# The order of a recurrent mixer's stages: second group's inverse and keys before the first group's chunks, first output projection before the second group's chunks

## The chip, the cores and the metric

The kernel runs on one core of one Trainium2 chip. The metric is the device time of one execution in microseconds (us), the median of several runs. The profiled execution is one further run, with its own time.

The engines are called PE (TensorE, matrix products), DVE (VectorE), ACT (ScalarE), POOL (GpSimd) and SP (SyncE, which issues DMAs here). Each takes its instructions strictly in the order in which they stand in its queue, and waits on semaphores for the others.

## The reference

A trunk of two layers over 256 tokens of width 1024. Each layer is a half-weighted SwiGLU feed-forward, a mixer, and a second feed-forward, each behind an RMS norm. The change concerns the mixer of the second layer, a gated delta recurrence with 16 heads of 64:

```python
r, k, v = xr @ w_r, xk @ w_k, xv @ w_v          # xr, xk, ...: token-shift lerps of h
w = -softplus(-(w0 + tanh(xw @ w1) @ w2)) - 0.5  # decay
a = sigmoid(a0 + (xa @ a1) @ a2)
g = sigmoid(xg @ g1) @ g2                        # gate
# per head, over the tokens:
sa = S @ a_t
S = S * w_t + sa * b_t + v_t * k_t
y_t = S @ r_t
y = group_norm(y) + sum(r * k * r_k) * v
return (y * g) @ w_o
```

## The kernel before

The 256 tokens are two halves of 128, the 1024 columns of the mixer two *groups* of 512 (8 heads each). The recurrence is computed in chunks of 64 tokens: inside a chunk the steps are solved by an inverse of a triangular matrix, and from chunk to chunk a 64x64 state per head is carried. All four chunks of one group are one chain; the two groups are independent of each other until the output projection.

The work of this mixer is cut into *stages*, each a Python call that emits its instructions. `ORDER` (line 32) is a string of stage names; `trunk` runs them one after the other in that order (the table of names is the dictionary `do` in it). From this program order a scheduler lays out the queue of each engine, and fills one stage's waits with instructions of neighbouring stages. So ORDER sets only roughly what stands where, and the engines' queues are shown below where they matter. The names, with G the group and h the token half:

- `k`, `r`/`R`, `v`/`V`: the three projections (`c_project`); the capital is the second group's columns. The weights come as fp32 and are split into a high and a low part (ACT L213, DVE L218 or POOL L216), and each product is three matmuls (L223 to L225). `v` also copies the values by chunk (ACT L665).
- `L`, `g`: the small loras; `g` is the gate's (`c_gate`): lerps whose product is on ACT (L593) and whose add is on POOL (L595), and matmuls on L603.
- `oG`, `pGh`, `DG`: operands of group G (keys normalised, decays); ACT, DVE and POOL work with transposes on PE.
- `bGh`, `kGh`: Gram blocks of the chunks (`c_gram`, PE L719 and L726, masked by DVE on L802), first those with b (tile `gb`), then those with k (tile `gk`).
- `sG`: `c_blocks` stores the diagonal blocks of `gb` to DRAM (`ds`, SP L819) and loads them in another layout as `L` (L824). `tG`: `c_substitute` solves these small blocks on DVE (L839 to L849) and stores the result (`xd`, `xtd`, L855). `lG`: `c_load` (L867) loads it back, per half as X (tiles `xx` for group 0, `hT` for group 1) and its transpose (`b`). `dGh`: `c_rest` builds the inverse of a whole chunk from it, in four rounds of PE (L719) and DVE (one L881, three L890).
- `vGh`: the bonus term (`c_bonus`): POOL products (L693), a DVE sum (L900), and a POOL add (L902).
- `cGh`: the two chunks of half h (`c_chunk`). A chunk is a chain, done for two pairs of banks: PE makes W, ACT copies it (L929), PE makes u, DVE copies it (L934), PE makes the new state, DVE scales it (L946, L949); the output leaves by ACT (L959).
- `WG`: the output weights of group G (`c_weights`), 8 loads of 256 KB by SP (L1025) through three `hn` buffers, each split by ACT (L289) and DVE (L290) into tiles that hold operands of group 0 before (`b`, `k`, `a`, `gb`, `gk` for W0, and `xx`, `hT`, `k`, `V`, `ka`, `rc` for W1).
- `PGh`: what follows the recurrence (`c_post`): gate (PE L977, ACT L979), centring by a matmul (PE L985), square and variance (ACT L989, DVE L991, L992), norm (DVE L998, L999), transposes (PE L1001) and a split.
- `OhG`: the output projection of half h with the rows of group G (`c_out`), 24 matmuls (L223 to L225), accumulated over G into one accumulator per half; `ah`: adds it to the trunk and begins the last feed-forward for half h (norm, with transposes on PE L268).
- `X`, `Y`: give and take back memory of the weight rings of the feed-forward (`rings_open("base")` at Y), after which its weights (`raw`) can be loaded.

```python
            for n in ORDER.split():
                do[n]()
```

Of the kernel before, what the change touches and what calls it, by code (L numbers as in the profile page):

```python
# [28 lines left out]
QB = (0, 0)  # L29
QV = (0, 0)  # L30
NPT = 2
ORDER = 'L k o0 r p00 p01 R b00 b01 g s0 o1 p10 p11 v V t0 D0 D1 X b10 b11 s1 l0 d00 d01 k00 k01 t1 v00 v01 l1 c00 c01 k10 k11 v10 v11 d10 d11 W0 P00 P01 c10 c11 P10 O00 W1 P11 O01 O10 Y a0 O11 a1'
BIG = 8
ORDER_AB = 'I0 N1 K0 Q0 S0 P0 E0 F0 I1 K1 Q1 S1 P1 E1 F1 O0 B0 O1 B1'
ABP = (2, 3, 0, 1)
# [1009 lines left out]
def trunk(tc, A, out, stop=None):  # L1045
    with ExitStack() as ctx:
# [56 lines left out]
        with t.pool("pre") as t.pre:  # L1103
# [18 lines left out]
            def tail(h):  # L1122
                t.add_acc(h, t.cs["acc", h])
                t.ffn_begin(S[3], h, 3)
# [13 lines left out]
            for G in range(2):  # L1138
# [16 lines left out]
                do[f"a{G}"] = lambda h=G: tail(h)  # L1155
            for n in ORDER.split():
                do[n]()
# [23 lines left out]
```

## Time and profile before

| | us |
| --- | --- |
| median of 3 runs | 1120.92 (1120.82 to 1122.24) |
| profiled execution, its own time | 1116.97 |
| its span | 1115.2 |
| PE busy | 1048.2 (94%) |
| DVE busy | 638.6 (57%) |
| ACT busy | 501.6 (45%) |
| POOL busy | 216.7 (19%) |

The mean granted clock of PE is 0.981 of full speed. The span is the time from the first to the last instruction, and 1.77 us of the execution lie around it. A busy share is a mean over the whole span; the stages of the mixer that the change moves lie between about 700 and 925 us of it. In a timeline, a row has the start, the duration, the engine, the source line and the tiles of one or several equal instructions, and in brackets how long the engine was idle before and which engine's instruction ended that.

### The profile page before, as it was taken

What the parts mean: (1) busy time and instruction counts of PE and PEld (TensorE: products, weight loads), DVE (VectorE), ACT (ScalarE), POOL (GpSimd) and SP (SyncE); (2) the same over time, 40 slices, a digit from 0 to 9 for tenths busy, and PEclk for the clock granted to TensorE, in tenths of its full rate; (3) what the DMA queues carried; (4) which work ended last, traced back from release to release, by engine and by line L of the source; (5) the groups of instructions that cost most, each with busy time, mean ns of one, the idle gap of its engine ahead of it and who ended that gap; (6) DMA issues with size and microseconds to landing.
All of it is one profiled execution on the core that took longest, in us unless ns stands there. A gap on an engine that the chain in (4) does not pass through costs nothing.

```text
span 1115.2 us, 16407 instructions
## 1 busy us (share of the span) xinstructions
PE 1048.2 (94%) x6332; PEld 859.9 (77%) x6332; DVE 638.6 (57%) x922; ACT 501.6 (45%) x804; POOL 216.7 (19%) x203
## 2 busy tenths in 40 slices
PE   6999999999999999989999999998685899999998
PEld 5888887778788888778888877886684777888886
DVE  6655555665655554754556546787454648554542
ACT  6544444564544443544444435756023326543440
POOL 3101110341201010111011111635200523100100
PEclk9999999999999999999999999999798999999999
DMA  8765664552765554646556444651323027645631
GB/s 294 258 202 175 221 191 157 181 189 80 231 199 178 189 193 147 222 160 205 185 172 210 148 138 152 192 157 55 74 60 112 24 95 244 235 163 190 195 127 38
DMA packets 73695, 185.07 MB, mean 166 GB/s; under 512 B 24081, under 2 KB 24721, under 8 KB 73617
## 3 DMA queue, kind: packets, MB, share of 16 engines
q1 hardware_dynamic: 70304, 178.19, 49.6%
q10 hardware_dynamic: 3312, 5.83, 1.7%
q8 instruction: 50, 0.82, 0.3%
q14 instruction: 29, 0.23, 0.1%
HBM read 180.32 MB, written 3.67 MB: 165 GB/s over the span
## 4 chain that ended last, share of the span: by engine, by line
PE 82%; DVE 6%; DMA 4%; POOL 3%; issue 2%; ACT 2%; SPq 1%; ACTq 0%; DVEq 0%; POOLq 0%
PE gu L224 14%; PE gu L223 14%; PE gu L225 14%; PE acc L223 10%; PE acc L224 10%; PE acc L225 10%; PE tp L336 2%; PE acc L719 2%; DMA hn<-w_rkvo 1%; DMA row<-gain 1%; DVE wlo L218 1%; PE gu L719 1%; ACT whi L213 1%; PE acc L268 1%; DVE hn L262 1%
## 5 line engine op out<-in xcount | busy, mean ns | idle before, releaser
L218 DVE TENSOR_TENSOR wlo<-raw,whi 128x1024 fp32r<-128x1024 f32 x261 | 345.4, 1330 | 184.3 <-ACT whi L213 180.2
L213 ACT CAST whi<-raw 128x1024 fp32r<-128x1024 f32 x306 | 319.2, 1050 | 209.4 <-DMA raw<-w_gu 94.2
L223 PE MATMUL gu<-whi,xh 128*128 128x512 f32 x704 | 279.8, 398 | 1.6 <-ACT whi L213 1.6
L224 PE MATMUL gu<-wlo,xh 128*128 128x512 f32 x704 | 279.3, 397 | 0.8 <-DVE wlo L218 0.8
L225 PE MATMUL gu<-whi,xl 128*128 128x512 f32 x704 | 278.3, 396 | 0.0
L216 POOL TENSOR_TENSOR wlo<-raw,whi 128x1024 fp32r<-128x1024 f32 x45 | 109.0, 2423 | 607.3 <-ACT whi L213 573.7
L223 PEld LDWEIGHTS gu<-whi,xh 128*128 128x128 f32 x704 | 133.1, 189 | 28.9 <-ACT whi L213 2.0
L224 PEld LDWEIGHTS gu<-wlo,xh 128*128 128x128 f32 x704 | 133.1, 189 | 27.7 <-DVE wlo L218 1.2
L225 PEld LDWEIGHTS gu<-whi,xl 128*128 128x128 f32 x704 | 133.1, 189 | 26.8
L223 PE MATMUL acc<-whi,ah 128*128 128x512 f32 x352 | 138.5, 394 | 1.9 <-ACT ah L289 1.7
L224 PE MATMUL acc<-wlo,ah 128*128 128x512 f32 x352 | 137.3, 390 | 0.0
L225 PE MATMUL acc<-whi,al 128*128 128x512 f32 x352 | 130.8, 391 | 0.0
L331 ACT ACTIVATE t<-gu,rh 128x256 f32<-128x256 f32 x88 | 41.3, 471 | 97.2 <-PE gu L225 96.7
L290 DVE TENSOR_TENSOR al<-tp,ah 128x256 fp32r<-128x256 f32 x88 | 36.9, 420 | 82.7 <-ACT ah L289 82.7
L289 ACT CAST ah<-tp 128x256 fp32r<-128x256 f32 x88 | 32.3, 367 | 111.6 <-PE tp L336 107.0
L332 DVE SCALAR_TENSOR_TENSOR t<-t,gu 128x256 f32<-128x256 f32 x88 | 36.6, 418 | 75.8 <-ACT t L331 75.0
L223 PEld LDWEIGHTS acc<-whi,ah 128*128 128x128 f32 x352 | 66.1, 188 | 17.4 <-ACT ah L289 3.4
L224 PEld LDWEIGHTS acc<-wlo,ah 128*128 128x128 f32 x352 | 66.1, 188 | 14.4
L225 PEld LDWEIGHTS acc<-whi,al 128*128 128x128 f32 x352 | 65.9, 188 | 14.3
L224 PE MATMUL acc<-wlo,xh 128*128 128x512 f32 x160 | 65.2, 408 | 0.2 <-DVE wlo L218 0.2
L223 PE MATMUL acc<-whi,xh 128*128 128x512 f32 x160 | 63.3, 410 | 0.7 <-ACT xh L289 0.5
L225 PE MATMUL acc<-whi,xl 128*128 128x512 f32 x160 | 62.7, 398 | 0.1
(487 smaller groups left out, 1111.7 us busy)
## 6 DMA issues: line engine op xcount, KB each, us to landing
raw<-w_gu SPq DMA_DIRECT2D x176, 512.0 KB, 4.5
raw<-w_dn SPq DMA_DIRECT2D x88, 512.0 KB, 4.3
raw<-w_rkvo SPq DMA_DIRECT2D x24, 512.0 KB, 3.6
row<-gain ACTq DMA_DIRECT2D x22, 256.0 KB, 4.2
raw<-w_qp SPq DMA_DIRECT2D x8, 512.0 KB, 4.3
raw<-w_out SPq DMA_DIRECT2D x8, 512.0 KB, 3.6
hn<-w_rkvo SPq DMA_DIRECT2D x16, 256.0 KB, 2.8
ch<-chan SPq DMA_DIRECT2D x10, 256.0 KB, 5.1
```

Of the source, the lines that this page charges most:

```text
L213: nc.scalar.copy(out=hi, in_=raw)
L216: nc.gpsimd.tensor_tensor(out=lo, in0=raw, in1=hi.bitcast(F32), op=ALU.subtract)
L218: nc.vector.tensor_tensor(out=lo, in0=raw, in1=hi.bitcast(F32), op=ALU.subtract)
L223: mm(out, xh, wh, start=start, stop=False)
L224: mm(out, xh, wl, start=False, stop=False)
L225: mm(out, xl, wh, start=False, stop=stop)
L289: self.nc.scalar.copy(out=hi, in_=src)
L290: self.nc.vector.tensor_tensor(out=lo, in0=src, in1=hi.bitcast(F32), op=ALU.subtract)
L331: nc.scalar.activation(out=t, in_=gu[:, :256], func=AF.Tanh, scale=rh)
L332: nc.vector.scalar_tensor_tensor(out=t, in0=t, scalar=1.0, in1=gu[:, :256], op0=ALU.add, op1=ALU.mult)
L336: nc.tensor.transpose(ps[:, j, :], t[:, j * 128:(j + 1) * 128], self.ident)
L719: self.nc.tensor.matmul(out[rs], a[rs], b[rs], start=start, stop=stop)
```

## The change

One line is changed, the string that orders the stages of the recurrent mixer.

```diff
--- before.py
+++ after.py
@@ -29,7 +29,7 @@
 QB = (0, 0)
 QV = (0, 0)
 NPT = 2
-ORDER = 'L k o0 r p00 p01 R b00 b01 g s0 o1 p10 p11 v V t0 D0 D1 X b10 b11 s1 l0 d00 d01 k00 k01 t1 v00 v01 l1 c00 c01 k10 k11 v10 v11 d10 d11 W0 P00 P01 c10 c11 P10 O00 W1 P11 O01 O10 Y a0 O11 a1'
+ORDER = 'L k o0 r p00 p01 R b00 b01 s0 o1 p10 p11 v g V t0 D0 D1 X b10 b11 s1 l0 d00 d01 k00 k01 t1 k10 v10 v00 v01 l1 d10 k11 c00 c01 v11 d11 W0 P00 P01 O00 c10 c11 P10 O10 Y W1 P11 O01 a0 O11 a1'
 BIG = 8
 ORDER_AB = 'I0 N1 K0 Q0 S0 P0 E0 F0 I1 K1 Q1 S1 P1 E1 F1 O0 B0 O1 B1'
 ABP = (2, 3, 0, 1)
```

Three things move. The gate's lora `g` goes from in front of `s0` to behind the projection `v`. The second group's inverse and keys (`k10`, `v10`, `d10`, `k11`) go ahead of the first group's chunks `c00` and `c01`. The output projection of token half 0 with group 0 (`O00`) goes ahead of the second group's chunks `c10` and `c11`, and `O10` and `Y` ahead of `W1` and `P11`. The set of instructions is the same.

SP's queue, at the stores and loads around the two substitutions (`ds`, `L`: `c_blocks`; `xx` and `b`: `c_load(0)`, halves 0 and 1). Before:

```order
L867 DMA xx_6757<-xd 64x512 x2
L819 DMA ds<-gb_6668 64x8x64 x2
L867 DMA b_5783<-xtd 64x512 x2
L867 DMA xx_6762<-xd 64x512 x2
L867 DMA b_5786<-xtd 64x512 x2
L819 DMA ds<-gb_6711 64x8x64 x2
L824 DMA L<-ds 32x16x16 x4
```

and now:

```order
L867 DMA xx_6757<-xd 64x512 x2
L819 DMA ds<-gb_6668 64x8x64 x2
L867 DMA b_5783<-xtd 64x512 x2
L819 DMA ds<-gb_6711 64x8x64 x2
L867 DMA xx_6762<-xd 64x512 x2
L867 DMA b_5786<-xtd 64x512
L824 DMA L<-ds 32x16x16 x4
```

The second store of `ds` moved ahead of two pairs of loads; half of one pair now stands behind the loads of `L`.

PE's queue in the first chunk of group 0 (`W`, `u`, `kt`, `bt`, `gk` are c00's; `hT`, `b_6259` are d10's). Before:

```order
L719 MATMUL gu<-hT_7064,gb_6668 64x64 x9
L719 MATMUL acc_7108<-W,b_5783 64x64 x4
L719 MATMUL acc_7115<-V_6520,kt_6950 64x64
L719 MATMUL acc_7091<-u,bt_6133 64x64 x2
L719 MATMUL acc_7091<-V_6520,kt_6950 64x64 x2
L719 MATMUL acc_7091<-u,bt_6133 64x64 x2
L719 MATMUL acc_7115<-V_6520,kt_6950 64x64
L719 MATMUL acc_7125<-gk_6939,V_6520 64x64 x2
```

and now (`gu<-tmp`, `ms<-tmp` and `tp<-tmp` are d10's, `a_6216,k_6215` is k11's):

```order
L719 MATMUL acc_7275<-W,b_5783 64x64 x2
L719 MATMUL gu<-tmp 64x64 x8
L719 MATMUL ms<-tmp 64x64 x8
L719 MATMUL acc_7258<-u,bt_6133 64x64 x2
L719 MATMUL acc_7258<-V_6472,kt_6950 64x64 x2
L719 MATMUL acc_7258<-u,bt_6133 64x64 x2
L719 MATMUL acc_7275<-W,b_5783 64x64 x2
L719 MATMUL tp<-tmp 64x64 x8
L719 MATMUL gu<-tmp 64x64 x8
L719 MATMUL gu<-a_6216,k_6215 64x128 x8
L726 MATMUL ms<-ident,k_6215 64x64 x8
L719 MATMUL tp<-a_6216,k_6215 64x128 x8
```

Rounds of d10 and the first Gram blocks of k11 now stand between the W, u and state products of the first chunk.

PE's queue at the end of the mixer, at P11's first transposes (`ident,tmp`; P11's centring stands some rows ahead of each piece). Before:

```order
L223 MATMUL acc_8242<-gk_7681,xh_7746 128x512
L224 MATMUL acc_8242<-gk_7681,xh_7746 128x512
L225 MATMUL acc_8242<-gk_7681,xl_7747 128x512
L223 MATMUL acc_8242<-gk_7682,xh_7746 128x512
L224 MATMUL acc_8242<-gk_7682,xh_7746 128x512
L225 MATMUL acc_8242<-gk_7682,xl_7747 128x512
L268 MATMUL acc_8285<-ident,hn 128x128 x4
L268 MATMUL acc_8293<-ident,hn 128x128 x4
L1001 MATMUL ms<-ident,tmp 128x128 x2
L223 MATMUL acc_8241<-xx_8139,xh_8202 128x512
L224 MATMUL acc_8241<-xx_8139,xh_8202 128x512
```

and now:

```order
L224 MATMUL acc_7762<-rc_8204,xh_8124 128x512
L225 MATMUL acc_7762<-ka_8203,xl_8125 128x512
L268 MATMUL acc_8285<-ident,hn 128x128 x4
L223 MATMUL gu<-whi,xh_8273 128x512
L224 MATMUL gu<-wlo,xh_8273 128x512
L268 MATMUL acc_8293<-ident,hn 128x128 x4
L225 MATMUL gu<-whi,xl_8275 128x512
L223 MATMUL gu<-whi,xh_8273 128x512
L224 MATMUL gu<-wlo,xh_8273 128x512
L225 MATMUL gu<-whi,xl_8275 128x512
L1001 MATMUL ms<-ident,tmp 128x128 x2
```

Before, 22 output matmuls stood between the centring and P11's first transposes; now eight do, with six of the feed-forward (`whi`, `wlo`) behind the norm's transposes (`ident,hn`).

## Rows read from the trace of the kernel before

**Rows 1.** The page, part 4: the chain that ended last, share of each engine.

```profile
PE 82%; DVE 6%; DMA 4%; POOL 3%; issue 2%; ACT 2%; SPq 1%; ACTq 0%; DVEq 0%; POOLq 0%
```

**Rows 2.** Busy us of PE, weight loads, DVE, ACT, GpSimd; clock; DMA, by stretch.

```profile
740.00:760.00 20.00, 19.42 (x89) 14.25 (x89) 17.76 (x46) 13.47 (x31) 4.63 (x5) 1.00 0.45 115
860.00:880.00 20.00, 14.13 (x266) 11.85 (x266) 14.52 (x31) 7.02 (x17) 12.53 (x12) 0.78 0.13 42
871.26:919.95 48.69, 46.00 (x576) 37.18 (x576) 25.64 (x58) 12.99 (x35) 15.98 (x21) 1.00 0.21 66
920.00:930.00 10.00, 7.67 (x29) 6.02 (x30) 10.00 (x10) 7.07 (x11) 6.27 (x6) 0.83 0.52 161
```

**Rows 3.** The same columns (PE, weight loads, clock), instructions of line L603 alone.

```profile
736.00:743.00 7.00, 4.37 (x32) 3.80 (x32) 1.00 0.51 146
```

**Rows 4.** Timeline of SP's DMA issues: start, us, engine, line, operation, tiles, count.

```profile
792.10 1.23 SPq L867 DMA_DIRECT2D b<-xtd  x2
793.44 1.29 SPq L819 DMA_DIRECT2D ds<-gb  x2
```

**Rows 5.** Timeline of DVE; in brackets the idle time before and its releaser.

```profile
787.92 0.69 DVE L802 TENSOR_TENSOR gb<-gu,m_si 128x512 f32<-128x512 f32 x1 [0.62 <-PE gu L719]
...
801.37 0.16 DVE L839 TENSOR_TENSOR pr<-L,XL 128x2 f32<-128x2 f32 x1 [6.43 <-DMA L<-ds]
...
814.69 0.69 DVE L849 TENSOR_REDUCE XL<-tmp 128x64 f32<-128x512 f32 x1
...
846.86 0.29 DVE L934 COPY u<-acc 128x128 f32<-128x128 f32 x1 [0.17 <-PE acc L719]
```

**Rows 6.** Timeline of GpSimd (POOL), the second group's bonus chain.

```profile
781.53 1.28 POOL L902 TENSOR_TENSOR vb<-vb,ch 128x512 f32<-128x512 f32 x1 [5.47 <-DMA ch<-chan]
```

**Rows 7.** Timeline of PE: k01's Gram, d10's start, d11, c10's start.

```profile
815.76 1.09 PE L719 MATMUL acc<-a,k 64*64 64x128 f32 x16 [1.55 <-DVE b L890]
816.68 0.63 PE L726 MATMUL acc<-ident,k 64*64 64x64 f32 x16
817.15 1.04 PE L719 MATMUL acc<-a,k 64*64 64x128 f32 x16
...
824.42 0.69 PE L719 MATMUL gu<-hT,gb 64*64 64x64 f32 x8 [0.23 <-DMA hT<-xd]
...
862.55 1.12 PE L719 MATMUL gu<-tmp 64*64 64x64 f32 x16 [5.00 <-DVE tmp L890]
...
871.26 0.45 PE L719 MATMUL ms<-W,b 64*64 64x64 f32 x8 [0.61 <-ACT W L929]
```

**Rows 8.** Timeline of ACT: a weight split, a P01 copy, c10's first W.

```profile
862.46 0.62 ACT L289 CAST V<-hn 128x512 fp32r<-128x512 f32 x1 [1.01 <-DMA hn<-w_rkvo]
...
869.45 0.60 ACT L989 ACTIVATE tmp<-acc 128x512 f32<-128x512 f32 x1 [2.10 <-PE acc L985]
...
870.93 0.28 ACT L929 COPY W<-tp 128x128 f32<-128x128 f32 x1
```

**Rows 9.** Timeline of PE: P11, end of the output projection, start of the feed-forward.

```profile
904.41 1.05 PE L985 MATMUL gu<-centre,Pt 128*128 128x128 f32 x8
...
911.31 0.38 PE L1001 MATMUL ms<-ident,tmp 128*128 128x128 f32 x2
...
919.33 0.40 PE L224 MATMUL acc<-rc,xh 128*128 128x512 f32 x1
919.56 0.39 PE L225 MATMUL acc<-ka,xl 128*128 128x512 f32 x1
921.55 0.51 PE L223 MATMUL gu<-whi,xh 128*128 128x512 f32 x1 [1.61 <-ACT whi L213]
...
923.27 0.80 PE L224 MATMUL gu<-wlo,xh 128*128 128x512 f32 x1 [0.77 <-DVE wlo L218]
923.86 0.63 PE L225 MATMUL gu<-whi,xl 128*128 128x512 f32 x1
924.29 0.63 PE L223 MATMUL gu<-whi,xh 128*128 128x512 f32 x1
```

## The prediction

> **What bounds the kernel now.** I read the chain of waits first: of the chain that ended last, 82% is TensorE (PE) [rows 1]. So a re-ordering can pay only where PE does not work, and the second view, the busy time of each engine by stretch, says where that is [rows 2]: from 740 to 760 us PE is busy 19.42 of 20 us, from 871.26 to 919.95 it is busy 46.00 of 48.69, but from 860 to 880 only 14.13 of 20, at a granted clock of 0.78. All stages that the new order moves lie between 736 and 925 us. The rest of the kernel is the same code with the same neighbours, so I take it at its old time.
>
> The third view is the timeline of single engines. It gives three places where PE waits for a chain that the order decides:
> - Group 1's inverse (stages s1, t1, l1). SP, the sync engine's DMA queue, stores the second `ds` half at 793.44 [rows 4], though its Gram block was ready on DVE at 788.61 (787.92 and 0.69) [rows 5]. It was held by the loads of c_load(0) that stand before it in the queue. The substitution starts when L lands (801.37, DVE idle 6.43 before) and ends at 815.38 [rows 5]; d10 begins on PE at 824.42 [rows 7].
> - The start of group 1's chunks. PE waits 5.00 us for one add of c_rest at 862.55 and begins c10 at 871.26 [rows 7]. Its first W copy on ACT (870.93) comes after the P00 and P01 copies, one of which waited 2.10 us for PE at 869.45 [rows 8], and after the last split of output weights.
> - The tail. P11's centring matmul starts at 904.41 and its transposes at 911.31; PE fills the 6.9 us between with output-projection matmuls, and goes on with them to 919.95 (919.56 and 0.39) [rows 9].
>
> **The change, part by part** (its profiled execution is 1116.97 us, 3.95 under the median of the runs, 1120.92; I make the sum against the first).
>
> 1. *Gate lora behind the v projection.* Its 32 matmul records are PE's work for 4.4 us [rows 3], and these go from in front of group 0's values. At most 4.4 us are gained. At least nothing: DVE, whose adds feed the same stretch, is busy 17.76 of 20 us there [rows 2], and the substitution t0 ends in DVE's order, not PE's. I take 1.8, a little under the middle, since DVE has only 2.2 us free in that stretch. The lerp's last add on GpSimd now stands in group 1's bonus chain, right behind an instruction that waits 5.47 us for a DMA and that, at the same 128x512, takes 1.28 us [rows 6]; I take 1.2 for the add. The Gram block behind this chain in DVE's order is then 0.4 to 1.2 us later against t0's end, which is covered: SP reaches its store only later still (next part). If that cover goes, it costs 1.2.
>
> 2. *SP's order.* The second `ds` store now has one load pair in front of it in place of three (an xx and a b pair move behind). The step from such a pair to the next issue is 1.34 us, 792.10 to 793.44 [rows 4]: 2.6 us gained. The loads that move back belong to d01; they still start before 794, and d01 comes behind d00. Together with part 1, L lands 4.4 us earlier, the substitution ends at about 811.0, and d10 starts at about 820.4, 4.0 us earlier (0.4 kept back for the GpSimd add). Bounds: 0 (gb late by the GpSimd add and by PE's order) and 7.0 (2.6 plus all of 4.4).
>
> 3. *d10, k10, k11 in front of c00.* PE now runs eight groups of d10 inside and ahead of the first chunk, each of 16 records of 64x64, 0.47 us by the step from 816.68 to 817.15 [rows 7]: 3.8 us. Of k11 there are two groups of 0.92 (815.76 to 816.68) and one of 0.47: 2.3 us. Before, 1.7 us of d10 stood there. So 4.4 us of PE come in front of the first state update, of which I count 4.0, because some lies in the chunk's own waits. That takes back all that part 2 gained: c01 ends where it ended, near its last u copy at 846.86 [rows 5]. Bounds: 0 (all in gaps) and 6.5 (four rounds that each wait a full hop to DVE, 1.6 us by the wait of 1.55 on c_rest's add at 815.76 [rows 7]).
>
> 4. *The start of c10.* The output weights land in tiles of group 0's operands, so they still follow c01. What changes is ACT's and DVE's order: P00's copies now stand between the splits, and d11's adds ahead of the last ones, so the 5.00 us wait at 862.55 and the 2.10 us wait at 869.45 fall away. W now stands before the last two splits, right behind the one of V, which ends at 863.08 (862.46 and 0.62). Four copies for P00 and P01 of 0.6 us go in front of it (865.5), c10's first matmul comes 0.33 us behind W as before (871.26 less 870.93) [rows 7, 8], and 0.5 for the rest of their waits on PE: c10 starts at 866.3 in place of 871.26, 5.0 us earlier. Bounds: 0 (the copies pull in their old waits) and 7.3 (W at 863.6, one copy behind V).
>
> 5. *From c10 to the end of the output projection.* Counted by rows, PE has the same instructions to do on both sides: 46.0 us, with 2.7 us of waits before [rows 2]. New is how little stands under P11. Of the output matmuls between its centring and its transposes, only eight are left, at 0.233 us (919.33 to 919.56 [rows 9]), 1.9 us, in place of 22. The last output matmul of token half 0 also moves to right before its norm, whose transposes PE must wait for. The 6.9 us are thus covered by 1.9 and 0.8 of centring: 4.2 us bare. With 1.3 us at c10's start: 866.3 + 46.0 + 5.5 = 917.8, against 919.95: 2.1 us gained. Bounds: the bare time may be 0 (feed-forward matmuls fill it) or 6.
>
> 6. *Start of the feed-forward.* PE idles 1.61 and 0.77 us at 921.55 and 923.27 and then steps at 0.43 us per matmul, 923.86 to 924.29 [rows 9]. With weights released a little earlier I take back half of the idle time, 1.2 us; bounds 0 and 2.4.
>
> Sum: 2.1 + 1.2 = 3.3 us off, 1113.7 for a profiled execution, **1117.6 us** as a median. A measurement of this kernel tells a change of about 0.2%, 2.24 us, from none.
>
> The clock speaks against the change. The rows show it: after those two waits the same matmul steps at 0.43 us in place of 0.233 [rows 9], with the granted clock of 920 to 930 at 0.83 [rows 2]; eight such steps cost 1.6 us. A bare wait of 4.2 us in front of the last output matmuls can do the same there: the sum would be 3.3 less 1.6, 1.7 us gained, 1119.2. The Trainium skill, in "TensorE: Matmul & The Clock Gate", section "HAM oscillation — how this bites in real kernels", says that a PE that waits for data between bursts falls back to its lower clock and pays the climb each time. The trace agrees in the stretch behind 921.55. Whether the new wait under P11 does so is not shown here.
>
> **The rivals.**
> - *No change.* The tail gives the lead back: the bare P11 wait at 4.2 us with the slow steps behind it (1.6), and nothing gained at the feed-forward's start (1.2). 3.3 − 1.6 − 1.2 = 0.5 us gained, 1120.4. For it: from 871 to 920 PE is nearly full, so only 2.7 us of waits can go there, and the order brings in a new one. Against it: the 7.1 us of waits that part 4 takes away lie before this stretch.
> - *Slower: the inverse of half 0 chokes the first chunks.* d10's rounds stand in DVE's order between the u copies of c00. If each costs its hop, 6.5 us are lost in part 3 in place of 4.0, and if the GpSimd add of part 1 and DVE's fill leave nothing of part 1, c01 ends 1.8 + 2.5 = 4.3 us later. The output weights wait for its tiles, so all of part 4 moves: the gain of 3.3 becomes a loss of 1.0, and with the slow steps 2.6, and with nothing at the feed-forward's start 3.8: 1124.7. It decides against the change once c01 ends after about 850.2. For it: PE waited on c_rest's adds before, 1.55 us at 815.76 and 5.00 at 862.55 [rows 7]. Against it: the long one of these came from splits that stood between, and none do in c00.
> - *Much faster: the P11 wait is filled.* Feed-forward matmuls of the first weight block do stand between P11's centring and its transposes in PE's order. If the norm of half 0 is ready for them, the 4.2 us go: 7.5 us gained, 1113.4. Against it: half 0's last output matmul now stands just before, and the norm's chain over ACT and DVE starts only there.
> - *The change doesn't do what it says* is excluded for the order itself; the order of instructions on PE, SP, ACT and DVE differs as listed above.
>
> **How the numbers follow.** Forecast 0.42 (own range 1115.5 to 1119.5), no change 0.24, slower 0.21, much faster 0.13. The forecast lies 1.1 us inside the bound for faster (1118.7), so some of it falls to no change: faster 0.52, same 0.27, slower 0.21. The range goes from 1112.0, a little under the fast rival, to 1124.7, the slow one; the unknown bounds of parts 2 to 5 lie within it.
>
> **What would show each step.** Part 1: L603 behind the v matmuls, and t0's L849 some 1.8 us earlier. Part 2: the second `ds` store straight after one b pair, L on DVE near 797, L849 of t1 near 811. Part 3: the first u copy of c00 early, but c01's end near 847. Part 4: c10's first W copy near 866 and no 5 us wait on `tmp`. Part 5: PE idle 4 us after P11's centring. Wrong it would be if c01 ends after 850, if c10 starts no earlier than 870, or if the P11 wait is absent.

## The result and the profile after

The median went from 1120.87 to 1126.04 us (8 runs each): a ratio of 1.0052 with a 95% interval of [1.0034, 1.007], so **slower by 0.5%**, 5.2 us. The forecast was 1117.6 and faster. The profiled execution after took 1126.33 us (span 1124.5), close to its median; the one before lies 3.9 us under its own. Differences between the two traces (9.4 us at the start of the last feed-forward) are therefore larger than the difference of the medians. They are read below for where the time lies, and the ratios for how much it is. Both traces reach the mixer at the same time: the last transposes (L336) of the feed-forward ahead of it stand at 660.09 us before and at 659.93 after. One run further down, of e14_after_nopool, took 1333.48 us at a granted clock of 0.747 and is left out of its ratio.

The page after, parts 1 and 4 (busy us and share by engine; the chain that ended last):

```profile
PE 1054.5 (94%) x6332; PEld 863.8 (77%) x6332; DVE 649.6 (58%) x922; ACT 501.8 (45%) x804; POOL 221.7 (20%) x203
PE 82%; DVE 7%; DMA 3%; ACT 2%; issue 2%; SPq 2%; POOL 1%; ACTq 0%; DVEq 0%; POOLq 0%
```

The shares answer [rows 1] and show nearly nothing: PE is still 82% of the chain. But PE is busy 6.3 us longer with the same 6332 matmuls, and that is the first hint at its clock. The stretches of [rows 2] tell more (columns as there):

```profile
740.00:760.00 20.00, 18.40 (x146) 15.08 (x147) 11.77 (x18) 10.99 (x26) 5.69 (x6) 0.85 0.48 114
860.00:880.00 20.00, 9.79 (x103) 6.36 (x104) 17.42 (x24) 8.62 (x17) 13.16 (x10) 0.64 0.38 118
872.02:930.60 58.58, 51.66 (x576) 40.48 (x576) 27.93 (x61) 14.47 (x37) 15.72 (x20) 0.88 0.21 68
920.00:930.00 10.00, 9.44 (x37) 7.24 (x38) 5.22 (x11) 2.38 (x4) 1.46 (x4) 0.83 0.52 154
```

Two places got worse. From 740 to 760 us DVE's work fell from 17.76 to 11.77 us and PE's clock from 1.00 to 0.85. From c10's first matmul to the end of the output projection (third row) PE needs 58.58 us in place of 48.69 for the same 576 matmuls, at a mean granted clock of 0.88 in place of 1.00.

DVE after, with the ends of the two substitutions (L849) and the last u copy of c01, which answer [rows 5]:

```profile
709.87 4.58 DVE L590 SCALAR_TENSOR_TENSOR hn<-xx,mu,hT 128x128 f32<-128x128 f32 x5
...
734.78 4.53 DVE L290 TENSOR_TENSOR xl<-hn,xh 128x512 fp32r<-128x512 f32 x2
...
743.18 0.68 DVE L802 TENSOR_TENSOR gb<-tp,m_si 128x512 f32<-128x512 f32 x1
...
749.67 0.69 DVE L802 TENSOR_TENSOR gb<-gu,m_si 128x512 f32<-128x512 f32 x1 [2.09 <-PE gu L719]
...
786.91 0.67 DVE L849 TENSOR_REDUCE XL<-tmp 128x64 f32<-128x512 f32 x1
...
805.45 0.17 DVE L839 TENSOR_TENSOR pr<-L,XL 128x2 f32<-128x2 f32 x1 [4.64 <-DMA L<-ds]
...
818.88 0.69 DVE L849 TENSOR_REDUCE XL<-tmp 128x64 f32<-128x512 f32 x1
...
853.92 0.29 DVE L934 COPY u<-acc 128x128 f32<-128x128 f32 x1 [0.17 <-PE acc L719]
```

The same places before:

```profile
698.18 1.14 DVE L590 SCALAR_TENSOR_TENSOR hn<-xx,mu,hT 128x128 f32<-128x128 f32 x4
...
706.60 1.28 DVE L290 TENSOR_TENSOR xl<-hn,xh 128x512 fp32r<-128x512 f32 x2
...
734.58 0.68 DVE L802 TENSOR_TENSOR gb<-tp,m_si 128x512 f32<-128x512 f32 x1
...
738.51 0.69 DVE L802 TENSOR_TENSOR gb<-gu,m_si 128x512 f32<-128x512 f32 x1 [0.81 <-PE gu L719]
740.04 1.80 DVE L590 SCALAR_TENSOR_TENSOR hn<-xx,mu,hT 128x128 f32<-128x128 f32 x3 [0.83 <-PE ms L603]
...
781.47 0.67 DVE L849 TENSOR_REDUCE XL<-tmp 128x64 f32<-128x512 f32 x1
```

So group 0's first and last Gram blocks are masked at 743.18 and 749.67 (before 734.58 and 738.51), t0 ends at 787.58 (before 782.14), L lands at 805.45 (801.37), t1 ends at 819.57 (815.38), and c01's last u copy is at 853.92 (846.86). Everything is late from the first of these on.

SP after, at s1, which answers [rows 4]:

```profile
796.93 1.30 SPq L819 DMA_DIRECT2D ds<-gb  x2
798.28 1.28 SPq L867 DMA_DIRECT2D xx<-xd  x2
799.61 1.74 SPq L867 DMA_DIRECT2D b<-xtd  x1
801.47 2.10 SPq L824 DMA_DIRECT2D L<-ds  x4
```

The second store of `ds` is issued 9.35 us behind t0's end (796.93 less 787.58) in place of 11.30, but three loads stand between it and those of L. L lands 17.9 us behind t0's end, before 19.2.

PE after, first group 0's Gram blocks, then the start of c10 (which answers [rows 7, 8]), then P11 ([rows 9]):

```profile
739.96 1.12 PE L726 MATMUL gu<-ident,b 64*64 64x64 f32 x16 [3.96 <-DVE b L786]
743.32 1.97 PE L719 MATMUL gu<-a,b 64*64 64x128 f32 x16 [1.60 <-DVE k L786]
...
867.82 2.07 PE L977 MATMUL acc<-l,sg 128*128 128x512 f32 x2 [3.46 <-ACT tmp L979]
...
872.02 0.69 PE L719 MATMUL ms<-W,b 64*64 64x64 f32 x8 [1.50 <-ACT W L929]
...
875.34 0.69 PE L1001 MATMUL acc<-ident,tmp 128*128 128x128 f32 x2 [1.78 <-DVE tmp L999]
878.04 0.77 PE L223 MATMUL acc<-b,xh 128*128 128x512 f32 x1 [2.01 <-DVE tmp L992]
...
913.86 1.05 PE L985 MATMUL gu<-centre,Pt 128*128 128x128 f32 x8
...
918.71 0.65 PE L268 MATMUL acc<-ident,hn 128*128 128x128 f32 x4 [1.94 <-DVE hn L262]
...
922.31 0.63 PE L223 MATMUL gu<-whi,xh 128*128 128x512 f32 x1
922.74 0.63 PE L224 MATMUL gu<-wlo,xh 128*128 128x512 f32 x1
...
923.59 0.39 PE L1001 MATMUL ms<-ident,tmp 128*128 128x128 f32 x2
```

PE waits 3.96 and 1.60 us for DVE at the Gram blocks. c10 starts at 872.02, not at 866.3. The 5.00 us wait on L890 is gone, but P00's gate matmul (L977) waits 3.46 us and c10 itself 1.50 us for ACT, and two more waits (1.78, 2.01), for DVE's work of the stages P00 and P01, fall into c10's first links. Under P11 PE waits 1.94 us for the norm, then steps at 0.43 us through the feed-forward's matmuls (922.31 to 922.74), and the transposes come 9.73 us behind the centring, before 6.90.

How fast PE ran in the first 10 us of c10, before and after (columns as in [rows 2]):

```profile
871.26:881.26 10.00, 8.10 (x204) 6.97 (x204) 9.05 (x24) 2.49 (x9) 8.01 (x10) 1.00 0.01 2
```

```profile
872.02:882.02 10.00, 6.21 (x74) 4.89 (x75) 8.50 (x15) 1.99 (x5) 5.89 (x7) 0.50 0.07 26
```

Before, PE was busy 8.10 us at full clock (2.4 GHz); after, 6.21 us at half (1.2 GHz). In work at full speed that is, by this estimate, 8.1 against 3.1: **5.0 us lost here**. In the 10 us ahead of c10 PE had been busy 4.23 us after and 7.29 us before.

### The profile page after: what moved, and what is told of

Read it like the earlier page. It is cut to its first block, busy times and chain, and to the rows that moved or that the text cites. A ratio compares the mean times of both kernels' runs of the same rounds, so it can differ in the third digit from the quotient of the medians.

```text
span 1124.5 us, 16409 instructions
## 1 busy us (share of the span) xinstructions
PE 1054.5 (94%) x6332; PEld 863.8 (77%) x6332; DVE 649.6 (58%) x922; ACT 501.8 (45%) x804; POOL 221.7 (20%) x203
## 4 chain that ended last, share of the span: by engine, by line
PE 82%; DVE 7%; DMA 3%; ACT 2%; issue 2%; SPq 2%; POOL 1%; ACTq 0%; DVEq 0%; POOLq 0%
PE gu L223 14%; PE gu L224 14%; PE gu L225 14%; PE acc L223 10%; PE acc L224 10%; PE acc L225 10%; PE acc L719 2%; PE tp L336 2%; PE gu L719 1%; DVE wlo L218 1%; DMA hn<-w_rkvo 1%; ACT whi L213 1%; PE acc L268 1%; PE tp L719 1%; DVE pr L839 1%
## 5 line engine op out<-in xcount | busy, mean ns | idle before, releaser
L216 POOL TENSOR_TENSOR wlo<-raw,whi 128x1024 fp32r<-128x1024 f32 x45 | 111.3, 2473 | 608.5 <-ACT whi L213 601.6
L290 DVE TENSOR_TENSOR al<-tp,ah 128x256 fp32r<-128x256 f32 x88 | 37.0, 420 | 78.5 <-ACT ah L289 78.5
```

The lines of the kernel that those rows point to most:

```text
L216: nc.gpsimd.tensor_tensor(out=lo, in0=raw, in1=hi.bitcast(F32), op=ALU.subtract)
L290: self.nc.vector.tensor_tensor(out=lo, in0=src, in1=hi.bitcast(F32), op=ALU.subtract)
```

## The experiments

Each kernel is the one before with the edit shown; ratios are to that one on the same chip. The diffs of `ORDER` show its stage names, one run of names a line; where nothing else is shown, the string alone is changed. The question of the first four: which of the three moves costs the time. The theory after the result was that the gate's move makes group 0's Gram blocks late and all else follows; the rivals were the inverse among the first chunks, and the tail.

**The gate's lora alone** (e1_gate).

```diff
 b00 b01
-g
 s0 o1 p10 p11 v
+g
 V
```

> Only the gate's lora is moved behind the v projection; the rest of the order is that of before. Theory T (the tail reorder costs it: in the changed kernel the stretch from c10's first matmul to the output projection's last takes 58.58 us in place of 48.69): within 2 us of before, because the lateness of t0's end (786.91 against 781.47) had shrunk to 0.76 us at c10's start. Theory G (the gate's move costs it, and the late front makes the tail late): 4 to 6 us slower than before. Both expect t0's last reduction near 786 to 787 and PE waits of about 4 and 1.6 us on the second Gram operands near 740.

Measured: 1129.24 us, ratio 1.0095 [1.0067, 1.0123]. The largest loss of the three. The Gram blocks are as late as after the whole change (last mask at 751.58), t0 ends at 788.98, c10 starts at 879.94.

**The inverse and keys alone** (e2_inverse).

```diff
 k00 k01 t1
+k10 v10
 v00 v01 l1
+d10 k11
 c00 c01
-k10 k11 v10
 v11
-d10
 d11
```

> Only k10, v10, d10 and k11 are moved ahead of group 0's chunks. Theory T: 0 to 3 us faster than before, c10's first matmul 0 to 5 us before 871.26 and the stretch to the output projection's end still 48 to 50 us. Theory G: the same. Theory I (the inverse in front of the first chunks is what makes group 0 late and with it the weights): 3 to 6 us slower, c01's end after 850.

Measured: 1117.41 us, 0.9995 [0.998, 1.001]: no change. PE at c10's start, and the W copy on ACT:

```profile
864.35 2.08 PE L977 MATMUL acc<-l,sg 128*128 128x512 f32 x2 [3.32 <-ACT tmp L979]
...
870.95 0.69 PE L1001 MATMUL acc<-ident,tmp 128*128 128x128 f32 x2 [3.87 <-DVE tmp L999]
871.57 0.69 PE L719 MATMUL ms<-W,b 64*64 64x64 f32 x8
```

```profile
868.36 0.27 ACT L929 COPY W<-tp 128x128 f32<-128x128 f32 x1
868.51 0.28 ACT L929 COPY W<-gu 128x128 f32<-128x128 f32 x1
```

W is copied at 868.51, 2.4 us earlier than before (870.93 [rows 8]), as part 4 wanted. But c10's matmul stands in PE's queue behind P00's transposes, and these wait 3.87 us for the norm (L999). So c10 starts at 871.57, before 871.26. This trace comes into the mixer 3.3 us later than the one before (its last L336 ahead of the mixer stands at 663.42 us, not 660.09; its granted clock is 0.98 from 100 to 200 us and from 400 to 500 us, where the trace before has 1.00). Counted from there c10 starts 3.0 us earlier and the last feed-forward's first transposes come 3.2 us earlier; of that nothing shows in the median.

**The tail alone** (e3_tail), and then its two halves (e5_o00, e6_o10).

```diff
 W0 P00 P01
+O00
 c10 c11 P10
-O00
+O10 Y
 W1 P11 O01
-O10 Y
 a0 O11 a1
```

> Only O00, O10 and Y are moved. Theory T: 4 to 8 us slower than before, with 55 to 60 us from c10's first matmul to the output projection's end, PE waiting on P00's transposes and multiplications and at half clock behind c10's start, and a bare wait under P11. Theory G: within 2 us of before, 48 to 52 us for that stretch, because P00 is then early enough.

Measured: 1124.37 us, 1.0052 [1.0035, 1.007]: by itself the ratio of the whole change. PE at P11:

```profile
906.67 1.06 PE L985 MATMUL gu<-centre,Pt 128*128 128x128 f32 x8
...
916.40 0.49 PE L1001 MATMUL ms<-ident,tmp 128*128 128x128 f32 x2
```

The gap is 9.73 us, as in the changed kernel. c10 starts at 868.49 and its first 10 us have the full clock (1.00); still it takes 54.93 us from there to the end of the projection, and PE is busy 49.61 of them, before 46.00 of 48.69. Counted in PE's queue, 8 output matmuls fill it in place of 22. The other 14, 3.3 us, now stand ahead of P11; yet from P11's centring to the end of the projection it takes 16.75 us, before 15.54. So the thin cover of P11 costs 1.21 + 3.3 = 4.5 us. It is the same in the changed kernel (913.86 to 930.61, 16.75). Not all of this is waiting: the mean granted clock of the 16.75 us is 0.90 in both, before 1.00.

`O00` ahead of `c10` alone:

```diff
 W0 P00 P01
+O00
 c10 c11 P10
-O00
 W1
```

> Of the tail only O00 is moved ahead of c10 and c11; O10 and Y stay behind O01. Theory Q (O00's matmuls stand in PE's queue between the links of c10's chain and lengthen it): 3 to 6 us slower than before, 54 to 55 us from c10's first matmul to the output projection's end in place of 48.69, as in the run with the whole tail moved. Theory U (what costs is P11, which loses its cover when O10 goes ahead of it): within 2 us of before, 48 to 51 us.

Measured: 1123.86 us, 1.0033 [1.0019, 1.0047]. From c10's first matmul to the end of the projection it takes 53.54 us, near the 54 to 55 of theory Q. `O10` and `Y` ahead of `W1` alone:

```diff
 c10 c11 P10 O00
+O10 Y
 W1 P11 O01
-O10 Y
 a0 O11 a1
```

> Of the tail only O10 and Y are moved ahead of W1 and P11; O00 stays behind P10. Theory U: 3 to 6 us slower than before, with a gap of 9 to 10 us between P11's centring and its transposes in place of 6.9 and a wait of about 2 us on the norm of token half 0. Theory Q: within 2 us of before.

Measured: 1118.57 us, 0.9989 [0.9975, 1.0003]. The loss comes with `O00`. Whether it arises between c10's links or under P11 is not told apart: with `O00` alone PE also waits 2.12 us for the norm (L999) ahead of P11's transposes. With `O00` alone, 14 output matmuls are left under P11 (22 before), with `O10` alone 21, with both 8.

**Gate and inverse, tail as before** (e4_no_tail).

```diff
 b00 b01
-g
 s0 o1 p10 p11 v
+g
 V t0 D0 D1 X b10 b11 s1 l0 d00 d01 k00 k01 t1
+k10 v10
 v00 v01 l1
+d10 k11
 c00 c01
-k10 k11 v10
 v11
-d10
 d11
```

> The gate and the inverse are moved as in the changed kernel, the tail is as before. Theory T: within 2 us of before, 48 to 50 us from c10's first matmul to the output projection's end. Theory G: 4 to 6 us slower than before, like the changed kernel.

Measured: 1124.17 us, 1.0045 [1.003, 1.0061]. The inverse, worth nothing by itself, takes back half of the gate's loss. With the gate alone c10 starts 26.2 us behind c01's last u copies (853.75 to 879.94), with both 17.4 us (854.28 to 871.72). But c10's first 10 us then run at half clock:

```profile
871.72:881.72 10.00, 6.18 (x74) 4.85 (x74) 8.50 (x15) 1.98 (x5) 5.89 (x7) 0.50 0.07 26
```

**Inverse and tail, gate as before** (e7_inv_tail).

```diff
 b00 b01 g s0 o1 p10 p11 v V t0 D0 D1 X b10 b11 s1 l0 d00 d01 k00 k01 t1
+k10 v10
 v00 v01 l1
+d10 k11
 c00 c01
-k10 k11 v10
 v11
-d10
 d11 W0 P00 P01
+O00
 c10 c11 P10
-O00
+O10 Y
 W1 P11 O01
-O10 Y
 a0 O11 a1
```

> The inverse and the whole tail are moved as in the changed kernel, the gate stays where it was. If the parts add: the tail's 0.5% and the inverse's nothing, 4 to 7 us slower than before. If the inverse in front lets the tail's order pay (c10 early enough for O00 to fill its waits): within 2 us of before or faster, and then the gate is all of the change's loss.

Measured: 1125.57 us, 1.0064 [1.0047, 1.0081]; c10's first 10 us:

```profile
871.88:881.88 10.00, 9.94 (x129) 7.71 (x129) 6.68 (x16) 2.65 (x8) 4.74 (x5) 0.77 0.01 2
```

With the gate at its old place the time is no better than that of the whole change (1.0052 [1.0034, 1.007]), although c10 begins here at 0.77 and not at 0.50. So the parts do not add up: gate 0.95%, inverse −0.05% and tail 0.52% would make 1.4%, and all three make 0.52%.

The next five ask **why the gate costs**, as it removes nothing and adds nothing. In the trace after, v's lerps (L590) and their splits (L290) stand on DVE between 702 and 739 us; before, they came behind the Gram blocks (L590 from 740.04, released by L603, the gate's matmul that reads `hn`). The gate's lerps use the same three `hn` buffers; once they stand behind v, v's get the buffers early. A run with more buffers was not made. And they are slow there: five L590 take 4.58 us (four took 1.14 at 698.18 before) and two L290 4.53 us (1.28 at 706.60 before). GpSimd at the same times:

```profile
708.46 3.73 POOL L216 TENSOR_TENSOR wlo<-raw,whi 128x1024 fp32r<-128x1024 f32 x1 [4.99 <-ACT whi L213]
712.16 1.34 POOL L767 TENSOR_TENSOR tmp<-ka,ch 128x512 f32<-128x512 f32 x1
...
734.75 2.34 POOL L216 TENSOR_TENSOR wlo<-raw,whi 128x1024 fp32r<-128x1024 f32 x1
737.05 1.71 POOL L693 TENSOR_TENSOR rc<-rc,ch 128x512 f32<-128x512 f32 x1
```

One by one, the stretched instructions end shortly behind GpSimd's. The first L590 took 2.48 us and ended at 712.35, where L216 ended at 712.19; the second took 1.39 and ended at 713.65, L767 at 713.51; the last three took 0.34 each. The two L290 took 2.86 and 1.75 and ended at 737.64 and 739.31, GpSimd's L216 and L693 at 737.09 and 738.76. So the rows look like waits for one whole instruction of GpSimd, and the second of each stands beside a product (L767, L693), not a split.

**The gate a little earlier, ahead of v** (e9_gate_half).

```diff
 b00 b01
-g
 s0 o1 p10 p11
+g
 v V
```

> The gate goes behind s0, o1, p10 and p11 but stays ahead of the v projection. Theory V (the gate's move is dear because v's sixteen lerps and four subtractions then come ahead on DVE, between 700 and 735 us, where DVE has no room, and group 0's Gram operands get late): within 2 us of before, the last of the first four Gram blocks near 738.5 as before. Theory W (the late gate itself is dear, its matmuls, and its adds on GpSimd beside the operands' products): 4 us slower or more, that block near 745 to 751.

Measured: 1129.06 us, 1.0077 [1.0057, 1.0098]. A miss for the theory, though the Gram blocks are on time (last mask at 740.41). PE between 740 and 760 us:

```profile
740.00:760.00 20.00, 9.40 (x46) 6.08 (x42) 12.68 (x30) 8.06 (x25) 5.70 (x9) 0.83 0.30 72
```

PE is busy 9.40 of 20 us, before 19.42 [rows 2]: the v projection itself now comes too late to fill this stretch. t0 even ends 14.1 us earlier (768.09), but group 1's Gram blocks come late (last mask at 803.29, before 787.92) and t1 ends at 826.70, before 815.38. Another loss of nearly the same size, so this run does not tell the theories apart.

**v's lerps early, the gate at its place** (e11_v_early). `w` runs v as far as its lerps.

```diff
+        if n == "v":
+            yield
...
+"w": lambda: next(v),
...
 b00 b01
+w
 g s0 o1 p10 p11 v V
```

> The lerps of the v projection become a stage of their own, ahead of the gate; the gate stays ahead of s0 and all else is as before. Theory V (the early lerps on DVE are what the gate's move costs): 5 us slower than before or more, PE waiting 3 to 4 us and 1.6 us for the second Gram operands, the last of the first four Gram blocks at 745 to 752. Rival (the gate's lateness itself costs it): within 2 us of before.

Measured: 1134.45 us, 1.0133 [1.0116, 1.0151]. DVE and PE (line numbers behind the added lines are 2 higher):

```profile
736.07 4.54 DVE L290 TENSOR_TENSOR xl<-hn,xh 128x512 fp32r<-128x512 f32 x2
...
751.56 0.69 DVE L804 TENSOR_TENSOR gb<-gu,m_si 128x512 f32<-128x512 f32 x1 [2.12 <-PE gu L721]
```

```profile
741.26 1.12 PE L728 MATMUL gu<-ident,b 64*64 64x64 f32 x16 [3.97 <-DVE b L788]
```

The same stretched pair, the same wait of 3.97 us, and the same late Gram block, with the gate untouched. So the early lerps of v are enough to make group 0's Gram blocks late; where the gate's 32 matmuls stand is not needed for it.

**The gate's move without GpSimd's splits** (e12_gate_nopool), and the kernel before without them as a control (e13_nopool).

```diff
-POOL_C = 6
+POOL_C = 600
```

(in e12_gate_nopool with the gate's move of e1_gate)

> As the run with the gate alone, but with no weight split of the mixer's projections on GpSimd: DVE does them too (1.2 us each alone). Theory C: a gain against that run, since two operations of GpSimd beside DVE's critical ones fall away; 3 to 7 us slower than before. Theory D: as slow or slower, 10 us over before or more.

Measured: 1123.59 us, 1.0038 [1.0022, 1.0055]. DVE in it:

```profile
712.55 1.13 DVE L590 SCALAR_TENSOR_TENSOR hn<-xx,mu,hT 128x128 f32<-128x128 f32 x4
...
736.32 1.28 DVE L290 TENSOR_TENSOR xl<-hn,xh 128x512 fp32r<-128x512 f32 x2
```

> The order of before, with no weight split of the mixer's projections on GpSimd. Theory C (GpSimd's splits stretch DVE only where v's early lerps meet them): within 2 us of before or slower, since DVE takes on some 1.2 us for each split and loses little beside them. Rival (the splits on GpSimd are dear in any order): 4 us faster or more, and then the same change in the gate's run says nothing of the gate.

Measured: 1130.08 us, 1.0094 [1.0077, 1.0112]. The kernel before loses 0.94% without GpSimd's splits. Its trace puts most of that behind c01, not where the splits were: c01's last u copy is at 849.15 (before 846.86), but from c10's first matmul (874.34) to the end of the projection it takes 59.77 us. Why it is so much longer there was not settled. With the gate moved, taking the splits away gains: 1.0095 to 1.0038. The pair L290 takes 1.28 us again, and t0 ends at 786.85. Counted from the last L336 ahead of the mixer that is 2.9 us later than before, with the splits (e1_gate) 6.5, and in the control, with the gate at its place, 2.7. So in that order most of t0's lateness comes with the splits on GpSimd beside DVE's early lerps. Of the Gram blocks' lateness they are only a part: the last mask is still at 747.49.

**The gate's lerp wholly on DVE** (e10_gate_dve), which takes its adds (L595) from GpSimd.

```diff
-SLOW = (5, 9)
+SLOW = (9,)
```

(with the gate's move of e1_gate)

> The gate is behind v as in the run with the gate alone, and its lerps are on DVE (16 more of L590, some 4.6 us) in place of ACT and GpSimd. Theory C (DVE's operations are stretched while GpSimd works: L590 x5 took 4.58 us beside GpSimd's work in place of 1.4): a gain against the run with the gate alone, 3 to 6 us slower than before. Theory D (DVE has too much to do from 700 to 740 us, whoever works beside it): as slow as that run or slower, 9 to 14 us over before.

Measured: 1127.39 us, 1.0072 [1.0052, 1.0092]. The interval overlaps that of e1_gate; the GpSimd add, which part 1 priced at up to 1.2 us, is not shown to cost anything.

**The whole change without GpSimd's splits** (e14_after_nopool: `POOL_C = 600` and the changed order).

> The changed kernel with no weight split of the mixer's projections on GpSimd. If theory C holds also in the whole: group 0's second operands without the 4 us wait, t0's end 4 us earlier than in the changed kernel; of the whole time perhaps nothing, since the tail alone with the inverse costs 6 us: 4 to 6 us slower than before. If the gate is all of the loss: within 2 us of before.

Measured: 1127.03 us, 1.0055 [1.0033, 1.0078], against 1.0052 with them. t0 ends at 786.42, 1.2 us earlier than in the changed kernel and not the 4 expected. What the splits cost with the gate moved alone does not show in the whole change.

**Towards a better order.** The inverse with c10 ahead of P00 and P01 (e8_inv_post):

```diff
 W0
+c10
 P00 P01
-c10
 c11
```

(with the inverse's move of e2_inverse)

> The inverse is moved as in the changed kernel, and P00 and P01 go behind c10; gate and tail as before. Theory R (with the inverse in front, c10 could start early, but its first W stands on ACT and PE behind P00 and P01, whose chain over DVE and GpSimd is late: waits of 3.3 and 3.9 us in the run with the inverse alone): c10's first matmul 3 to 5 us before 871.57, the whole 2 to 4 us faster than before. Rival (the output weights' splits on DVE and ACT bind c10 and P00 alike, in whatever order): within 2 us of before.

Measured: 1118.38 us, 0.9986 [0.9974, 0.9999]. c10's first matmul is at 872.27, not 3 to 5 us ahead of 871.57: theory R missed, and its rival (within 2 us of before) came. Then this with `O10` and `Y` ahead of `W1`, that is, the parts of the change that did not cost, with P00 and P01 behind c10 (e15_best), and the same with `POOL_C = 600` (e16_best_nopool):

```diff
 W0
+c10
 P00 P01
-c10
 c11 P10 O00
+O10 Y
 W1 P11 O01
-O10 Y
 a0 O11 a1
```

(with the inverse's move of e2_inverse)

> Gate where it was, O00 behind P10 as before; the inverse ahead of the first chunks, P00 and P01 behind c10, O10 and Y ahead of W1. If the small gains of the parts add (0.14% and 0.11%): 2 to 4 us faster than before. If they are one gain, or none: within 2 us.

Measured: 1116.87 us, 0.9979 [0.9964, 0.9994].

> As the run before, with no weight split of the mixer's projections on GpSimd. By theory C: no faster than that run. By its rival: 4 us faster than it.

Measured: 1122.13 us, 1.0026 [1.0011, 1.0041]. By these ratios e15_best is faster than both kernels, by 0.2% against the one before, just what can be told from nothing, and it is the best of sixteen tries. Its parts by themselves, 0.9986 and 0.9989, make 0.9975.

## Why the prediction was wrong, by its steps

The sum forecast 3.3 us off for the trace; 9.4 us came on (the feed-forward's first transposes, L336, at 944.72 against 935.30). In the medians it is 5.2 us. The miss stands in two terms. c10's start, which parts 1 to 4 put at 866.3, came at 872.02: 5.7 us. From there to the end of the projection part 5 took 46.0 + 5.5 = 51.5 us, and it was 58.58: 7.1 us. Each of the two moves behind them loses by itself (e1_gate 0.95%, e3_tail 0.52%), and with the gate left at its place the other two still lose 0.64% (e7_inv_tail).

- **Part 1 failed, and parts 2 to 4 were built on it.** Taken: 1.8 us gained, "at least nothing". Measured: t0 ends 5.4 us later (787.58 against 782.14), and the move alone costs 0.95%. The lower bound counted the matmuls that move and DVE's busy share, but not what the gate had held back: v's lerps, which waited for `hn` until the gate's matmul (L603) had read it. Released, these go ahead of the Gram blocks in DVE's order, beside GpSimd's splits; the same two L290 take 4.53 us in place of 1.28. e11_v_early shows that they do it without the gate, e12_gate_nopool that without the splits they are not stretched and 0.57% comes back. How the late Gram blocks become lost time is less clear: e10_gate_dve has them later still (last mask at 754.89) and loses 0.72%, e9_gate_half has them on time and loses 0.77%. The Trainium skill, in "GPSIMD Engine Reference", section "8. Key points", says that GpSimd shares its SBUF interfaces with VectorE and contends with VectorE instructions that have two SBUF inputs. Both stretched lines have two such inputs, and the rows agree.
- **Part 2 was right in kind, half in size.** L follows t0's end in 17.9 us, before 19.2: 1.4 us gained, where 2.6 were taken. The store itself gained 1.95 us; the loads moved behind it take the rest back before L's. With part 1 at its measured value L lands 4.1 us later and not 4.4 earlier.
- **Part 3 is not settled.** It took 4.0 us, to be paid by part 2, which did not pay. Its mechanism is in the queue: rounds of d10 stand between the u copies. Its size cannot be read from one trace. With the inverse alone c01's last u copy is 3.8 us later (850.68 against 846.86), but 3.3 of these had come ahead of the mixer. Counted from the last L336 ahead of the mixer, c01 ends 0.5 us later in e2_inverse, 2.9 in e8_inv_post, 3.4 in e7_inv_tail and 5.8 in e15_best, all with the same order as far as c01. With the order of before as far as c01, it ends 2.9 us later in e5_o00 and 3.0 earlier in e3_tail. In the changed kernel the last u copy is 7.1 us late, past the 850 that the text set as a sign that it is wrong; 4.2 of these are there at t1's end (819.57 against 815.38).
- **Part 4 failed in its end.** The stretch from c01's last u copy to c10 did shrink, from 24.4 us (846.86 to 871.26) to 18.1 (853.92 to 872.02), by more than the 5.0 taken, and the 5.00 us wait is gone. But c10 started 0.8 us later, since c01 ended 7.1 us later. What its lower bound named came in part, "the copies pull in their old waits": P00's and P01's chain over ACT and DVE makes PE wait 3.46 and 1.50 us (in e2_inverse 3.32 and 3.87) where it had waited for L890.
- **Part 5 failed in its 46.0 us of work.** The wrong step was "the same instructions to do on both sides: 46.0 us". The count of instructions is the same, the PE time is 51.66 us in the changed kernel, 49.61 in e3_tail and 49.79 in e7_inv_tail. In the changed kernel c10 begins at half clock: 5.0 us are lost in its first 10. For P11 the part said 4.2 us bare, and 4.5 were measured, in e3_tail as in the changed kernel; the nearness is in part luck, for the gap was 9.73 us and not 6.9, and the 4.5 hold slow steps, which the prediction had set apart at 1.6. Together 5.0 and 4.5 are most of the 9.9 us by which the stretch grew. The 5.0 are two things: PE is busy 1.9 us less, for it waits 1.78 and 2.01 us for DVE's work of P00 and P01 between c10's links, and what it does runs at half speed (3.1). In e3_tail c10 has the full clock, and the loss there is of another kind.
- **The clock at c10** goes with the inverse's move. Each kernel with the inverse moved shows a clock under 1.00 there: PE was busy 4.23 us of the 10 ahead of c10 in the change and 4.24 in e4_no_tail, and c10's first 10 us have a granted clock of 0.50; it was busy 3.38 in e7_inv_tail (0.77) and 3.35 in e2_inverse (0.82). With the inverse at its place it was busy 7.29 before, 6.96 in e3_tail and 7.08 in e6_o10, and c10 has 1.00; in e1_gate it was busy 8.15, and c10 has 0.83. e13_nopool does not fit: the inverse is at its place, PE was busy 6.92, and c10 has 0.71. Rounds of the inverse (d11's L719 at 862.55 [rows 7]) stood in that stretch before. The Trainium skill, in "TensorE: Matmul & The Clock Gate", section "HAM oscillation — how this bites in real kernels", says that a PE which waits between bursts falls to its lower clock. The prediction set this against the end of the tail; the rows agree there too (steps of 0.43 us from 922.31), but the larger price stood at c10.
- **Part 6 was right in its number**: from the end of the projection to L336 it takes 14.11 us, before 15.35, so 1.2 gained. Its reason, weights released earlier, is not shown: e2_inverse takes 13.29 with the tail as before.
- **The rivals.** The slower one had the right sign and nearly the size (1124.7, also the end of the range, 1.3 under the median measured), but that is luck, for its cause was wrong: the inverse among the first chunks is neutral by itself (e2_inverse). The filled P11 wait did not come: the feed-forward's matmuls came, but behind 1.94 us of waiting, at half clock.

What stays open. Which moves cost is measured; by what path they cost is shown only in part. That the gate alone costs 0.95%, and nothing on top of inverse and tail (e7_inv_tail), is measured, not explained. e4_no_tail shows part of it, as c10 follows c01 8.8 us sooner with the inverse moved. Why the tail then takes the rest was not settled. That the clock at c10 is what eats the early start was read from the traces; a run that fills PE ahead of c10 without moving anything else was not tried.

## What to carry to other kernels

When a stage moves, ask what it held back: which buffers it shared, and which instructions take its place on the engine in front. Before two traces are compared, line them up at a point ahead of the change; here that took back 3.3 of 3.8 us in one reading. A bound of "at least nothing" for a mere move needs the same proof as a gain. And a stretch of PE that is taken as so many instructions also needs its clock: look at what PE does ahead of it.

## What the hardware showed that was not expected

- VectorE beside GpSimd: two L290 of 128x512 took 4.53 us with GpSimd at work, 1.28 without; five L590 of 128x128 took 4.58 us, where four took 1.14. Four of these seven were stretched, and each ended within 0.6 us behind an instruction of GpSimd.
- Taking GpSimd's share of the splits away costs 0.94% in one order and gains 0.57% in another (e13_nopool; e12_gate_nopool against e1_gate).
- Executions of kernels with the same order of stages as far as c10 reach it at times that differ by 6.2 us (e3_tail 868.49, e5_o00 874.71, with the last L336 ahead of the mixer at 660.53 and 660.33), though medians can be told apart at about 0.2%. One trace places the losses; it does not size them to a microsecond.
